# A hybrid RG-LRU and gated DeltaNet trunk on one core: new durations in the table from which a generator writes the order of the work

## The chip, the core and the metric

The kernel runs on one NeuronCore of one Trainium2 chip. The metric is the device time of one launch in microseconds. The engines are TensorE (PE, and PEld for its weight loads), VectorE (DVE), ScalarE (ACT), GpSimd (POOL) and SyncE (SP), which issues all the transfers. Each engine takes its instructions in the order in which the program lists them, and an instruction whose operand is not ready holds up everything behind it on that engine.

## The reference, cut to what matters

Two layers over 2048 frames of width 1024, then a last RMSNorm. Each layer is x = x + gate * Mixer(RMSNorm(x) * (1 + scale) + shift), where shift, scale and gate come from a linear map of SiLU(c).

```
# layer 0, RG-LRU
xb, zg = split(h @ in_w)                          # 1024 -> 2 * 1024
xb = causal_conv4(xb) + conv_b
r, i = sigmoid(blockdiag(xb) + gate_b)            # 8 blocks of 128 x 128
a = exp(-8 * r * softplus(-lam))
hseq = scan(h_t = a_t * h_{t-1} + sqrt(1 - a^2) * (i * xb))
out = (hseq * silu(zg)) @ out_w

# layer 1, gated DeltaNet, 8 heads of 128
q, k, v = silu(causal_conv4(h @ in_w[q, k, v]));  z, a_in, b_in = h @ in_w[z, a, b]
per chunk: A = strict_lower(beta * k k^T * decay);  T = (I + A)^-1
           v_new = T(beta v) - T(beta k e^g) S;  o = (q e^g) S + (q k^T * decay) v_new
           S = S * e_last + k_dec^T v_new
out = (rmsnorm(o) * silu(z)) @ out_w
```

All inputs and outputs are fp32.

## The kernel before

Every large matrix product is made of three products of fp32r halves (high by high, high by low, low by high), each 128x128 by 128x512, accumulated in a PSUM tile over eight blocks of 128: 24 products for one tile of 128x512. They are the line `pe.matmul` of `products` (L667); the tile is `mm` in the input projections and `mmo` in the output projections. A *job* is one such tile. The first layer has 64 jobs for its input and 32 for its output projection, the second 128 and 32. The tokens come in two halves `u` of 1024, each in two groups `i` of 512.

What hangs on a job of the first layer: ScalarE copies `mm` to `xe` (`extend`, L727; POOL copies the carry of four columns, L725 and L730), POOL makes the first tap of the convolution and VectorE the other three (`taps`, L715, the tile `xf1`); ScalarE rounds it to `xh` (L765), VectorE makes the rest `xl` (L768), and six gate products `pg` (L774) on TensorE use both. Then come the activations, the scan on VectorE (L805) and the product with the other branch (`tz`, L752). Beside that, `row_halves_thread` accumulates the condition columns on VectorE (`acc`, L412) and reduces them with small products (L280, L423); VectorE and POOL split the normalised input of the next half into `hh` and `hl` (L570, L576).

In the second layer a job of the kinds q, k and v goes through the same convolution (`xf`) to `qt`, `kt`, `vt` (L975). For a head, `key_thread` transposes the key on TensorE (`pk`, L1094), makes `pkk` (L1129) and the decayed matrix `ac`; `inverses_thread` inverts its 32x32 blocks by substitution on VectorE, 62 dependent steps (`ttmp`, `tblk`, L1249 and L1252); `levels_thread` merges them; `query_thread` makes `pqk` (L1214). `recurrence_thread` then goes over eight blocks `m` of 128 tokens for each half: two products `pp` with the state (L1369, L1370), `zt` on VectorE (L1378), `py` (L1386), `yt` on ScalarE (L1392), two products `pS` (L1398, L1399), and the new state on VectorE (L1411), which the next `pp` needs.

**What sets the order.** The program has no loops on the chip. Python threads (generators) describe the work, and the class `Weave` runs them at build time: each `yield "dve", 0.605` says that the next instructions take VectorE for 0.605 us by the table, each `yield slots[...]` asks for a buffer, each `yield ev(...)` waits for another thread. `run` always takes the thread that can start first by this reckoning, and among equals the one with the lower priority number; the recurrences have 0, the projections 9. What it takes is emitted, and so the four engines and the transfer queue each get their fixed order. Nothing of this reckoning is left at run time: there, semaphores make an instruction wait for its operands. So the table's numbers set where an instruction stands in its queue, and nothing else. The names in capitals are the commonest durations: STT and EV a 128x512 VectorE instruction, CP a 128x512 ScalarE copy, TR a 128x128 transpose, MM a 128x512 product and M4 a 128x128 fp32 product. LAG is the time from an instruction's end until its result counts as usable.

Buffers matter too: PSUM has two tiles each of `mm`, `tp`, `c` and `d`, so a job cannot start before the job two before it has been copied out.

## Time and profile before

| | |
|---|---|
| three runs | 1982.22, 1989.81, 1986.4 us; median 1986.4 |
| the profiled execution | 1980.38 us, span 1978.6 us |
| busy: PE, PEld | 1846.2 us (93%), 1500.3 us (76%) |
| busy: DVE, ACT, POOL | 1475.7 us (75%), 1046.7 us (53%), 724.1 us (37%) |
| DMA | 322.77 MB, mean 163 GB/s |
| granted TensorE clock | 0.985 |

A busy PE is a sum of modelled, overlapping durations, so what counts on TensorE is where it has nothing running, and what ended that idle time. In the views, "PE pg L774 <- DVE xl L768" reads: TensorE stood idle before an instruction of line 774 that writes `pg`, and the last thing to come was VectorE's `xl` of line 768. The chain that ended last goes through TensorE for 46% of the span, VectorE 21% and DMA 10%.

### The profile page before, as it was taken

Reading aid. Unit: us, or ns where it says so; the run is one execution under the profiler, and the core shown is the slowest. Engines: PE = TensorE matmul, PEld = TensorE weight load, DVE = VectorE, ACT = ScalarE, POOL = GpSimd, SP = SyncE. Lnnn points to the kernel's source line nnn. Section 1 sums busy time; section 2 is a strip of 40 time slices with the busy share of each in tenths; the row PEclk is TensorE's granted clock in tenths of the full one; section 3 lists DMA queues with packets and bytes.
Section 4 is the critical chain, followed back from the end, with each engine's and each line's share of the span. In section 5 each row is a group of like instructions: output and inputs, shape, how many; then the busy total and the mean of one; then the engine's idle time right before and its main releaser. Section 6 shows DMA issues by size and latency. Waiting matters only on the chain.

```text
span 1978.6 us, 31398 instructions
## 1 busy us (share of the span) xinstructions
PE 1846.2 (93%) x10286; PEld 1500.3 (76%) x10286; DVE 1475.7 (75%) x3171; ACT 1046.7 (53%) x2555; POOL 724.1 (37%) x1215
## 2 busy tenths in 40 slices
PE   6998889999998998898989999999999999999998
PEld 3776667787787777777777778777888888878887
DVE  6788798887644567778977898567778778877654
ACT  3655567666411236465555555555656566654321
POOL 4555664444200135345344544333333334311101
PEclk9999999999999999999999999999999999999999
DMA  8355655654578724547764457455465555577751
GB/s 334 103 157 158 223 168 169 200 178 153 175 198 210 225 74 140 145 114 176 189 161 130 119 125 191 128 147 147 119 152 147 131 133 140 149 219 221 225 186 64
DMA packets 511724, 322.77 MB, mean 163 GB/s; under 512 B 371268, under 2 KB 439236, under 8 KB 511560
## 3 DMA queue, kind: packets, MB, share of 16 engines
q1 hardware_dynamic: 511560, 320.77, 57.4%
q8 instruction: 81, 1.33, 0.3%
q14 instruction: 83, 0.68, 0.1%
HBM read 219.93 MB, written 100.73 MB: 162 GB/s over the span
## 4 chain that ended last, share of the span: by engine, by line
PE 46%; DVE 21%; DMA 10%; issue 6%; ACT 6%; POOL 5%; SPq 5%; DVEq 0%; POOLq 0%; ACTq 0%
PE mm L667 21%; PE mmo L667 12%; DVE xf L715 6%; DMA raw<-in_w 2%; DVE ttmp L1249 2%; DVE tblk L1252 2%; PE pg L774 1%; DMA xt<-x_d 1%; SPq L1187 1%; SPq L512 1%; DVE acc L412 1%; PE pp L1369 1%; PE pS L1398 1%; PE pkk L1129 1%; PE pS L1399 1%
## 5 line engine op out<-in xcount | busy, mean ns | idle before, releaser
L715 DVE SCALAR_TENSOR_TENSOR xf<-xe,cw_s,xf 128x512 f32<-128x512 f32 x384 | 331.4, 866 | 46.7 <-POOL xf L958 24.1
L649 POOL TENSOR_TENSOR wlo<-raw,whi 128x1024 fp32r<-128x1024 f32 x48 | 120.6, 2512 | 99.7 <-ACT whi L643 81.2
L1249 DVE TENSOR_TENSOR ttmp<-blk,tblk 128x60 f32<-128x60 f32 (+24 forms) x496 | 118.3, 238 | 24.9 <-DMA blk<-blk_d 11.5
L643 ACT CAST whi<-raw 128x1024 fp32r<-128x1024 f32 x96 | 100.4, 1045 | 64.5 <-DMA raw<-in_w 54.7
L1252 DVE TENSOR_TENSOR tblk<-tblk,ttmp 128x60 f32<-128x60 f32 (+24 forms) x496 | 122.3, 247 | 10.0 <-POOL tblk L1243 0.2
L730 POOL COPY carry<-xe 128x4 f32<-128x4 f32 x128 | 40.3, 315 | 239.2 <-ACT xe L727 237.1
L727 ACT COPY xe<-mm 128x512 f32<-128x512 f32 x128 | 73.9, 578 | 74.0 <-PE mm L667 73.0
L667 PE MATMUL mm<-hh_('in2', 0)_5201,whi 128*128 128x512 f32 x256 | 105.0, 410 | 4.1 <-ACT xe L727 4.1
L667 PE MATMUL mmo<-oh,yh 128*128 128x512 f32 x256 | 101.1, 395 | 7.8 <-DVE xr L922 7.2
L667 PE MATMUL mm<-hh_('in2', 1)_12203,whi 128*128 128x512 f32 x256 | 105.2, 411 | 2.8 <-ACT xe L727 2.8
L667 PE MATMUL mm<-hh_('in2', 0)_5424,whi 128*128 128x512 f32 x256 | 103.7, 405 | 2.1 <-ACT xe L727 1.5
L667 PE MATMUL mm<-hh_('in2', 0)_5201,wlo 128*128 128x512 f32 x256 | 105.3, 411 | 0.0
L667 PE MATMUL mm<-hl_('in2', 0)_5425,whi 128*128 128x512 f32 x256 | 104.9, 410 | 0.0
L667 PE MATMUL mm<-hl_('in2', 0)_5202,whi 128*128 128x512 f32 x256 | 104.6, 409 | 0.0
L667 PE MATMUL mm<-hh_('in2', 1)_12379,wlo 128*128 128x512 f32 x256 | 104.4, 408 | 0.0
L667 PE MATMUL mm<-hh_('in2', 1)_12203,wlo 128*128 128x512 f32 x256 | 104.4, 408 | 0.0
L667 PE MATMUL mm<-hh_('in2', 0)_5424,wlo 128*128 128x512 f32 x256 | 104.0, 406 | 0.0
L667 PE MATMUL mm<-hl_('in2', 1)_12204,whi 128*128 128x512 f32 x256 | 103.8, 405 | 0.0
L667 PE MATMUL mm<-hl_('in2', 1)_12380,whi 128*128 128x512 f32 x256 | 103.2, 403 | 0.0
L667 PE MATMUL mm<-hh_('in2', 1)_12379,whi 128*128 128x512 f32 x256 | 103.1, 403 | 0.0
L667 PE MATMUL mmo<-oh,oh 128*128 128x512 f32 (+1 forms) x264 | 102.0, 386 | 0.2 <-DVE tz L986 0.2
L667 PE MATMUL mmo<-ol,oh 128*128 128x512 f32 (+1 forms) x264 | 102.1, 387 | 0.0
(324 smaller groups left out, 5698.7 us busy)
## 6 DMA issues: line engine op xcount, KB each, us to landing
raw<-in_w SPq DMA_DIRECT2D x96, 512.0 KB, 4.2
araw<-in_ada_w SPq DMA_DIRECT2D x32, 512.0 KB, 4.4
xt<-x_d SPq DMA_DIRECT2D x32, 512.0 KB, 4.5
xt_d<-xb SPq DMA_DIRECT2D x192, 64.0 KB, 2.6
xk<-xt_d SPq DMA_DIRECT2D x24, 512.0 KB, 5.5
xt<-in_x SPq DMA_DIRECT2D x16, 512.0 KB, 4.9
ada<-in_ada_w SPq DMA_DIRECT2D x16, 512.0 KB, 9.1
y_d<-tz SPq DMA_DIRECT2D x32, 256.0 KB, 3.1
```

Source lines behind the costliest of these rows:

```text
L412: dve.scalar_tensor_tensor(acc, raw[:, k, :], ck, acc, ALU.mult, ALU.add)
L512: sp.dma_start(out=dst[c_], in_=tb[32 * c_:32 * c_ + 32])
L643: act.copy(hi, raw)
L649: pool.tensor_tensor(lo, raw, f(hi), ALU.subtract)
L667: pe.matmul(pt, lhsT=lhs[a][:, k, :], rhs=rhs[b][:, k, :], start=(k == 0 and n == 0), stop=(k == KT - 1 and n == 2))
L715: dve.scalar_tensor_tensor(xf, xe[:, 1 + j:1 + j + TC], wc[:, j:j + 1], xf, ALU.mult, ALU.add)
L727: act.copy(xe[:, 4:4 + TC], pt)
L730: pool.tensor_copy(out=carry, in_=xe[:, TC:TC + 4])
L774: pe.matmul(pg, lhsT=a[:, g, :], rhs=b, start=(q == 0), stop=(q == 2))
L1129: pe.matmul(pkk[:, b, :], lhsT=kc, rhs=kc, start=True, stop=True)
L1249: dve.tensor_tensor(tmp, blk[:, j, j + 1:32].unsqueeze(2).to_broadcast([P, r, c_]), t[:, j, 0:c_].unsqueeze(1).to_broadcast([P, r, c_]), A ...
L1252: dve.tensor_tensor(t[:, j + 1:32, 0:c_], t[:, j + 1:32, 0:c_], tmp, ALU.subtract)
```

## The change

The table of durations is replaced nearly everywhere, and TensorE's part of `Weave` gets two kinds of work. "pe" are the small products; "mm" the large ones, and an "mm" that comes behind a "pe" counts 0.087 us longer. Apart from the reckoning, only the matrix `middle` is moved: it was made by two POOL instructions at the start, in memory kept for the whole kernel, and is now made when the second layer's memory is opened, and `decay_thread` waits for it.

```
+    SWITCH = 0.087
+    ENGINE = {"mm": "pe"}
...
-                self.free[w[0]] = t + w[1]
-                th.t = t + w[1] + (w[2] if len(w) > 2 else self.LAG[w[0]])
+                dur = w[1]
+                if w[0] in ("pe", "mm"):
+                    if w[0] == "mm" and self.small:
+                        dur += self.SWITCH
+                    self.small = w[0] == "pe"
+                e = self.ENGINE.get(w[0], w[0])
+                self.free[e] = t + dur
+                th.t = t + dur + (w[2] if len(w) > 2 else self.LAG[e])
...
-    STT, EV, CP, TR, MM, M4 = 0.665, 0.605, 0.48, 0.109, 0.2163, 0.218
+    STT, EV, CP, TR, MM, M4 = 0.78, 0.61, 0.49, 0.112, 0.2275, 0.23
...
-            yield "pool", 0.14
+            yield "pool", 0.27
...
-        yield "dve", STT
+        yield "dve", 1.41
...
-            dur = 0.065 + r * c_ / 960.0
+            dur = 0.11 + r * c_ / 960.0
...
-                yield "act", 0.16
+                yield "act", 0.19
...
-    middle = cp.tile([P, P], F32, name="middle")
-    pool.tensor_copy(out=middle, in_=upper)
-    pool.tensor_scalar(middle[0:64, :], middle[0:64, :], -1.0, 0.0, ALU.add, ALU.add)
...
         enter("l2", "l2a")
+        middle = tile_([P, P], "middle", "middle")
+        pool.tensor_copy(out=middle, in_=upper)
+        pool.tensor_scalar(middle[0:64, :], middle[0:64, :], -1.0, 0.0, ALU.add, ALU.add)
+        w.set(ev("middle"), middle)
```

The four single prices are those of the carry copies in `extend` (0.14 to 0.27), the scan (0.665 to 1.41), a step of the substitution and `yt`. Left out are some thirty more prices of the same kind, most of them raised: the other VectorE instructions of the first layer from 0.605 to between 0.69 and 0.85, POOL's from 0.6 to 0.93 and the like, ScalarE's by a few hundredths, the four groups of small products in `levels_thread` from 0.38, 0.88, 0.4 and 0.9 to 1.1, 1.1, 1.0 and 1.1.

Line numbers below are those of each kernel's own text; up to L940 a line of the functions spoken of here stands 7 lines further down in the changed kernel, and from `decay_thread` on 12 or 13. The scan L805 is printed as SCALAR_TENSOR_TENSOR in the order and as TENSOR_TENSOR_SCAN in the profile.

How the order moves, first on VectorE in the first layer, around the fifteenth `xl`, from the last taps of its `xf1` to itself. Before:

```order
L715 SCALAR_TENSOR_TENSOR xf1_2238<-xe1_2217,cw1_s_97,xf1_2238 128x512 x2
L801 TENSOR_TENSOR tg_2127<-tg_2127,tg_2109 128x512
L805 SCALAR_TENSOR_TENSOR tg_2127<-th_2141,tg_2127 128x512
L412 SCALAR_TENSOR_TENSOR acc_2038<-araw_2247,c_col_92,acc_2038 128x512 x2
L801 TENSOR_TENSOR tg_2185<-tg_2185,tg_2177 128x512
L570 CAST hh_('in1', 1)_2265<-h_2286 128x512
L805 SCALAR_TENSOR_TENSOR tg_2185<-th_2196,hcar_104,tg_2185 128x512
L576 TENSOR_TENSOR hl_('in1', 1)_2266<-h_2286,hh_('in1', 1)_2265 128x512
L570 CAST hh_('in1', 1)_2265<-h_2292 128x512
L768 TENSOR_TENSOR xl_2316<-xf1_2238,xh_2299 128x512
```

And the same `xl` in the changed kernel:

```order
L722 SCALAR_TENSOR_TENSOR xf1_2269<-xe1_2240,cw1_s_94,xf1_2269 128x512
L577 CAST hh_('in1', 1)_2282<-h_2312 128x512
L759 SCALAR_TENSOR_TENSOR tz_2319<-tz_2319,mm_2244 128x512
L583 TENSOR_TENSOR hl_('in1', 1)_2283<-h_2312,hh_('in1', 1)_2282 128x512
L775 TENSOR_TENSOR xl_2342<-xf1_2269,xh_2324 128x512
```

The two scans and the two accumulations that stood between the last tap and `xl` now stand ahead of the taps; three instructions are left between.

Second on TensorE in the second layer, one step of a recurrence (`py`, then `pS`) in the second half of the tokens. Before:

```order
L1386 MATMUL py_14110<-zt_14095,ac_13111 128x128
L667 MATMUL mm_14098<-hh_('in2', 1)_12379,wlo_13712 128x512
L667 MATMUL mm_14098<-hh_('in2', 1)_12379,whi_13789 128x512
L667 MATMUL mm_14098<-hl_('in2', 1)_12380,whi_13789 128x512
L667 MATMUL mm_14098<-hh_('in2', 1)_12379,wlo_13712 128x512
L1398 MATMUL pS_14124<-yt_14115,kd_13021 128x128
L1399 MATMUL pS_14124<-yt_14115,at_13203 128x128
```

And the same step in the changed kernel:

```order
L1399 MATMUL py_14129<-zt_14120,ac_13085 128x128
L674 MATMUL mm_14075<-hl_('in2', 1)_12413,whi_13731 128x512
L674 MATMUL mm_14075<-hh_('in2', 1)_12412,wlo_13676 128x512
L674 MATMUL mm_14075<-hh_('in2', 1)_12412,whi_13731 128x512
L1411 MATMUL pS_14140<-yt_14132,kd_12983 128x128
L1412 MATMUL pS_14140<-yt_14132,at_13206 128x128
```

Three large products stand between `py` and `pS` where four stood.

More of the change, by code (lines that the diff above doesn't have):

```diff
@@ L75 @@
     LAG = {"pe": 0.2, "act": 0.3, "dve": 0.3, "pool": 0.2}
+    SWITCH = 0.087
+    ENGINE = {"mm": "pe"}
     def __init__(self):
         self.free = dict.fromkeys(("pe", "act", "dve", "pool", "sp", "dma"), 0.0)
+        self.small = True
         self.threads = []
@@ L108, in start @@
             return max(th.t, w.freed[last]) if last in w.freed else None
-        return max(th.t, self.free.get(w[0], 0.0))
+        return max(th.t, self.free.get(self.ENGINE.get(w[0], w[0]), 0.0))
     def run(self):
@@ L206, in trunk_kernel @@
     tags |= {t: ("l2", n) for t, n in {
-        "xe": 2, "xf": 2, "kt": KTN, "qt": QTN, "vt": 1, "ec": 3, "gr": 1, "ac": 4, "atn": 4, "kd": 4, "vn": 4,
+        "xe": 2, "xf": 2, "kt": KTN, "qt": QTN, "vt": 1, "ec": 3, "gr": 1, "middle": 1, "ac": 4, "atn": 4, "kd": 4, "vn": 4,
         "rq": 4, "nk": 4, "oo": 2, "tblk": 1, "ttmp": 1, "tf": 2, "zt": 2, "t2": 2, "yt": 2, "so": 2, "ro": 2,
@@ L210, in trunk_kernel @@
         "gs": 2, "eg": 2}.items()}
-    for t in ("xe", "xf", "vt", "ec", "gr", "ab", "gin", "gg", "spe", "spd"):
+    for t in ("xe", "xf", "vt", "ec", "gr", "middle", "ab", "gin", "gg", "spe", "spd"):
         tags[t] = ("l2a", tags[t][1])
@@ L457, in scale_thread @@
         put("ss", stok)
-        yield "dve", STT
+        yield "dve", 0.7
         dve.tensor_scalar(xt, xt, rs, None, ALU.mult)
@@ L559, in split_thread @@
         ttok = yield slots[tag]
-        yield "act", 0.665
+        yield "act", 0.71
         h = tile_([P, TC], tag, "h")
@@ L568, in split_thread @@
         else:
-            yield "dve", 0.33
+            yield "dve", 0.46
             dve.tensor_copy(out=hh[:, k, :], in_=h)
@@ L574, in split_thread @@
         else:
[L575 removed]
+            yield "dve", 0.75
             dve.tensor_tensor(hl[:, k, :], h, f(hh[:, k, :]), ALU.subtract)
@@ L728, in extend @@
         put("mm", mtok)
-        yield "pool", 0.14, 0.0
+        yield "pool", 0.27, 0.0
         pool.tensor_copy(out=carry, in_=xe[:, TC:TC + 4])
@@ L738, in conv1_thread @@
         ftok = yield slots["xf1"]
-        yield "pool", 0.76
+        yield "pool", 1.2
         xf = tile_([P, TC], "xf1", "xf1")
@@ L765, in gates_thread @@
         act.copy(xh, xf)
-        yield "dve", EV
+        yield "dve", 0.7
         xl = tile_([P, TC], "xr", "xl", F32R)
@@ L786, in gates_thread @@
         act.activation(tr, tr, AF.Exp, bias=sp4n[:, n:n + 1], scale=sp4n[:, n:n + 1])
-        yield "dve", EV, 0.13
+        yield "dve", 0.69, 0.13
         dve.scalar_tensor_tensor(th, tr, 1.0, th, ALU.add, ALU.mult)
-        yield "dve", EV
+        yield "dve", 0.69
         dve.scalar_tensor_tensor(tr, th, 2.0, th, ALU.subtract, ALU.mult)
-        yield "pool", 0.6, 0.0
+        yield "pool", 0.93, 0.0
         pool.tensor_scalar(th, th, -1.0, 1.0, ALU.mult, ALU.add)
-        yield "dve", EV
+        yield "dve", 0.85
         dve.scalar_tensor_tensor(ti, ti, 1.0, xf, ALU.add, ALU.mult)
@@ L806, in gates_thread @@
         put("th", htok)
-        yield "pool", 0.13
+        yield "pool", 0.42
         pool.tensor_copy(out=hcar[:, n:n + 1], in_=ti[:, TC - 1:TC])
@@ L810, in gates_thread @@
         tz, ztok = yield ev("tz", u, n, i)
-        yield "pool", 1.23
+        yield "pool", 1.42
         pool.tensor_tensor(tz, tz, ti, ALU.mult)
@@ L955, in conv2_thread @@
         ftok = yield slots["xf"]
-        yield "pool", 0.68
+        yield "pool", 0.72
         xf = tile_([P, TC], "xf", "xf")
@@ L1045, in decay_thread @@
         yield "pe", 1.1
+        middle = yield ev("middle")
         pgc = ps.tile([P, 3, NB * NH], F32, tag="tp", name="pgc")
@@ L1286, in levels_thread @@
         ctok = yield slots["c"]
-        yield "pe", 0.38
+        yield "pe", 1.1
         px = ps.tile([P, NTC, TB, 32], F32, tag="c", name="px")
@@ L1449, in outputs_thread @@
         for b in range(TB):
-            yield "act", 0.255, 0.0 if b < TB - 1 else 0.27
+            yield "act", 0.295, 0.0 if b < TB - 1 else 0.27
             act.activation(oo[:, b, :], oo[:, b, :], AF.Copy, scale=ro[:, b:b + 1])
```

28 lines of the change are left out of this document (13 added, 15 removed).

## Prediction

> **What bounds the kernel now.** I read the page first, then the stages, then who TensorE waited for, and last the order of time at the places where it waited longest.
>
> The page's span, busy shares and slices (TensorE):
>
> ```profile
> span 1978.6 us, 31398 instructions
> ...
> PE 1846.2 (93%) x10286; PEld 1500.3 (76%) x10286; DVE 1475.7 (75%) x3171; ACT 1046.7 (53%) x2555; POOL 724.1 (37%) x1215
> ...
> PE   6998889999998998898989999999999999999998
> ```
>
> TensorE is at work in 93% of the span, nothing else comes near, and the dips lie at the start, in the fourth to sixth digit and from the thirteenth to the twenty-first. The stages tell it in microseconds (columns: stage and length, then busy time of PE, PEld, DVE, ACT, POOL with their instructions, granted clock, DMA share, GB/s):
>
> ```profile
> 60.00:300.00 240.00, 209.07 (x852) 163.42 (x851) 202.52 (x238) 147.50 (x206) 143.84 (x137) 0.95 0.56 168
> 300.00:490.00 190.00, 184.79 (x806) 149.42 (x804) 159.63 (x199) 130.14 (x170) 84.55 (x97) 0.99 0.55 179
> 490.00:697.00 207.00, 195.92 (x841) 157.79 (x840) 113.79 (x150) 57.17 (x71) 30.16 (x36) 0.99 0.68 197
> 697.00:1240.00 543.00, 499.55 (x3175) 409.29 (x3174) 433.01 (x1149) 300.75 (x931) 239.93 (x437) 0.98 0.57 144
> 1240.00:1783.00 543.00, 528.02 (x3497) 436.77 (x3496) 412.05 (x1203) 329.60 (x1004) 178.15 (x412) 1.00 0.56 147
> 1783.00:1979.00 196.00, 188.45 (x971) 157.42 (x967) 113.88 (x151) 57.71 (x136) 21.53 (x56) 0.99 0.56 172
> ```
>
> The first two rows are the input projection of the RG-LRU layer, the third its output projection, the fourth and fifth the two halves of the DeltaNet layer, the last the final output projection. TensorE stands still for 240.0 - 209.1 = 31 us in the first row, 5 us in the second, 11 in the third, 543 - 499.6 = 43 us in the fourth, 15 in the fifth and 8 in the last. Only this standing time can be won by another order, since the products themselves stay; one row of the chain of waits prices them:
>
> ```profile
> 1832.16 139.53 PE mmo L667 x638
> ```
>
> 638 products with nothing waiting, the last 48 of them half as wide: 139.53 / (590 + 24) = 227 ns for one of 128x512. Below I count a place in TensorE's order in units of these 227 ns.
>
> Who TensorE waited for (us in total, times, longest):
>
> ```profile
> PE pg L774 <- DVE xl L768: 23.1, 13, 5.2
> ...
> PE pS L1398 <- ACT yt L1392: 9.1, 12, 1.6
> PE mm L667 <- ACT xe L727: 8.4, 5, 2.8
> PE pp L1369 <- DVE state L1411: 7.8, 6, 1.9
> ...
> PE pk L1094 <- DVE tblk L1252: 5.2, 4, 2.0
> PE adac L280 <- DVE acc L358: 4.8, 2, 2.5
> PE adapt L423 <- DVE acc L412: 3.9, 2, 2.8
> PE py L1386 <- DVE zt L1378: 3.9, 6, 1.6
> ...
> PE adapt L280 <- DVE acc L412: 3.4, 3, 1.7
> ```
>
> Most of it is one kind: a small product on TensorE stands in its in-order queue before VectorE (or ScalarE) has made its operand, and every large product behind it waits too. The sum of the rows with a VectorE or ScalarE cause here is 69.6 us.
>
> **The change, term by term.** All sums are against the profiled execution (1980.38 us, span 1978.6), which lies 6.0 us under the median of the three runs, 1986.4; I add the sum to that median, because after the change a median is compared too. The change adds no arithmetic and no transfer: TensorE has the same 8452 instructions, VectorE and the sync queue the same number. It moves them, moves two POOL instructions, and drops four loads of an activation table.
>
> Gate products (pg behind xl). The longest wait, in order of time on VectorE and then on TensorE:
>
> ```profile
> 272.93 0.75 DVE L715 SCALAR_TENSOR_TENSOR xf<-xe,cw_s,xf 128x512 f32<-128x512 f32 x1
> ...
> 275.46 2.55 DVE L412 SCALAR_TENSOR_TENSOR acc<-araw,c_col,acc 128x512 f32<-128x512 f32 x2
> ...
> 278.88 1.27 DVE L805 TENSOR_TENSOR_SCAN tg<-th,hcar,tg 128x512 f32<-128x512 f32 x1
> 280.07 0.66 DVE L576 TENSOR_TENSOR hl_('in1', 1)_2266<-h,hh_('in1', 1)_2265 128x512 fp32r<-128x512 f32 x1
> 280.65 0.41 DVE L570 CAST hh_('in1', 1)_2265<-h 128x512 fp32r<-128x512 f32 x1
> 280.99 0.68 DVE L768 TENSOR_TENSOR xl<-xf,xh 128x512 fp32r<-128x512 f32 x1
> ```
>
> ```profile
> 281.72 0.79 PE L774 MATMUL pg<-xl,gh 128*128 128x512 f32 x1 [5.16 <-DVE xl L768]
> 282.31 0.63 PE L774 MATMUL pg<-xh,gl 128*128 128x512 f32 x1
> ```
>
> The last tap of the convolution ends at 272.93 + 0.75 = 273.68, but xl, which TensorE stands waiting for, starts at 280.99: nine other VectorE instructions stand between them in the order, among them two of the accumulations L412 (2.55 us) and two scans. The generator had taps, accumulations and scans at 0.665 us each; the rows of a tap and an accumulation say otherwise (beside them a step of the inverse and an instruction with one operand in PSUM, for later):
>
> ```profile
> L715 DVE SCALAR_TENSOR_TENSOR xf<-xe,cw_s,xf 128x512 f32<-128x512 f32 x384 | 331.4, 866 | 46.7 <-POOL xf L958 24.1 <-POOL xf L741 17.0 <-POOL xe L721 2.2
> ...
> L1249 DVE TENSOR_TENSOR ttmp<-blk,tblk 128x60 f32<-128x60 f32 (+24 forms) x496 | 118.3, 238 | 24.9 <-DMA blk<-blk_d 11.5 <-DMA tt_d<-ttmp 2.4 <-POOL tblk L1243 1.6
> L412 DVE SCALAR_TENSOR_TENSOR acc<-araw,c_col,acc 128x512 f32<-128x512 f32 x56 | 50.6, 903 | 6.0 <-DMA araw<-in_ada_w 5.6
> ...
> L752 DVE SCALAR_TENSOR_TENSOR tz<-tz,mm 128x512 f32<-128x512 f32 x32 | 21.8, 680 | 11.2 <-ACT tz L750 8.4 <-issue 2.8
> ```
>
> 866 (L715) and 903 ns (L412) against 665, and 1.27 us for the scan at 278.88. With 0.78 (and 1.41 for the scan) the generator holds VectorE for longer, so the small product comes later among the large ones. At this place the order now leaves three VectorE instructions between tap and xl (by their rows L570 0.41, L752 0.68 and L576 0.66, 1.8 us instead of 7.3), and the 5.16 us should go. Over all 32 groups, the number of large products between the end of the projection and the pg that needs xl rises from 43.5 to 48.9 in the mean: 5.4 x 227 ns = 1.2 us more lead. If each of the 13 waits shrank by that, 13 x 1.2 = 15.6 us would go. But in the mean VectorE has as many instructions between tap and xl as before (2.6), and at nine of the 32 places the lead is shorter; priced place by place with the old times, new waits eat all and 1 us more. Between -15.6 and +1 I take -9, nearer to the first, because the longest wait is one that I can see go.
>
> Clock. After the 5.16 us the next two products last 0.79 and 0.63 us, and the granted clock of 60 to 300 us is 0.95: 5% of 240 us is 12 us. Fewer long waits give some of it back: 0 to -6, I take -2.
>
> Accumulations before the condition columns (L280, L423): 4.8 + 3.9 + 3.4 = 12.1 us in seven waits. Eight steps that are priced 0.115 us higher place the product 0.9 us later: up to -6; +2 if the longer lead only moves the column's users. I take -3.
>
> Key transposes (pk): 5.2 us in four waits behind tblk, the substitution inside the inverses. Its steps are 238 ns in the row L1249; the generator had 0.065 us plus a nanosecond per element and now has 0.11, still too little. The lead grows by 0.2 us in the mean, by over 1 us at most of the waiting places. From -8 to +6, I take -2.
>
> Recurrence, third product (pS behind yt). One step of it in order of time, on TensorE and then on ScalarE:
>
> ```profile
> 1399.84 0.38 PE L1386 MATMUL py<-zt,ac 128*128 128x128 f32 x2
> 1399.98 0.47 PE L667 MATMUL mm<-hh_('in2', 1)_12379,wlo 128*128 128x512 f32 x1
> 1400.30 0.39 PE L667 MATMUL mm<-hh_('in2', 1)_12379,whi 128*128 128x512 f32 x1
> 1400.52 0.40 PE L667 MATMUL mm<-hl_('in2', 1)_12380,whi 128*128 128x512 f32 x1
> ...
> 1400.99 0.38 PE L1398 MATMUL pS<-yt,kd 128*128 128x128 f32 x2
> ```
>
> ```profile
> 1400.26 0.28 ACT L1392 ACTIVATE yt<-py 128x128 f32<-128x128 f32 x1 [0.38 <-PE py L1386]
> ```
>
> pS starts 1400.99 - 1399.84 = 1.15 us after py, behind four large products; yt is done at 1400.54, so there are 0.45 us to spare. The generator now counts the first large product behind a small one as 0.087 us longer. That is real: it occupies 1400.30 - 1399.98 = 0.32 us here, the next 0.22. So it puts three products where four stood (72 of 120 places had four, now 63 have three), and 0.45 - 0.22 = 0.23 us are left. ScalarE is not always free:
>
> ```profile
>   PE py L1386: 30.2, 67
> ```
>
> In 67 of 128 cases ScalarE stood idle until py came; in the other 61 something else ran. If all 61 cost the lost product, 61 x 0.22 = +13 us; if the better table keeps ScalarE clear, the 9.1 us go. The twelve places that wait already lose 12 x 0.22 = 2.6; I take +3. The other two steps of the recurrence (py behind zt, 3.9 us; pp behind the state, 7.8) keep four products in most places, in the mean 0.07 and 0.12 us fewer: 120 x 0.19 = +23 at worst, -11.7 if all waits go, and I take 0, since neither table nor order says which.
>
> The rest at nothing, with what covers it. Exposed weight loads: the order has 550 returns from small to large products, before 555; five times 0.1 us is -0.5. Waits for PSUM (mm behind xe, 8.4 us): xe is priced 0.49 instead of 0.48, the distance between a bank's two uses is the same in the mean. Table loads:
>
> ```profile
> L797 ACT ACT_TABLE_LOAD x26 | 33.4, 1283 | 0.5
> ```
>
> 26 such loads before the square roots (53 in all) become 24 (49 in all): 4 x 1.283 = 5 us of ScalarE, which is 147.5 of 240 us busy there; between -5 and 0, taken as 0. The matrix `middle` is made by two POOL instructions that move from the kernel's start to the opening of the second layer, where POOL is busy 30.2 of 207 us; its user stands behind all of the decays' other work. Without that cover it would cost under 1 us.
>
> Sum: -9 - 2 - 3 - 2 + 3 + 0 = -13, so 1986.4 - 13 = 1973 us. 0.5% (10 us) is about what a measurement of this kernel can tell from no change, so this is just beyond it.
>
> **Rivals.**
>
> (A) The plan meets the chip. If nearer prices make most VectorE-caused waits go, half of the standing time in the two worst stages goes, (31 + 43)/2 = 37 us, with 6 us of clock: 1943. For it: the waits do name the instructions whose price was lowest against their rows. Against it: the leads in the second layer hardly grow (pk 0.2 us, the recurrence less than nothing).
>
> (B) Tight recurrences, slower. With three products behind py, a ScalarE that starts yt more than 0.23 us late stops TensorE; 61 of 128 cases are exposed: +13, and a third of the +23 of py and pp is +8: 1986 + 21 = 2007. It decides if the wait for yt doubles without the pg wait halving. Against it: at most places ScalarE starts yt at once.
>
> (C) Prices that change with the order. The row of xl (min/median/max) shows that one instruction has no one price:
>
> ```profile
> L768 DVE TENSOR_TENSOR xl<-xf,xh x32: 657/682/1745, 65.0 to 512.9; 128x512 fp32r<-128x512 f32 x32
> ```
>
> 657 to 1745 ns for the same tile, and the taps L715 take 866 ns where L752, with one operand in PSUM, takes 680. Something lengthens VectorE instructions with two SBUF operands by up to a microsecond, and a new order pairs them anew. The taps lose 384 x (866 - 680) = 71 us in all; a quarter more is 18 us of VectorE, of which I count the quarter of the taps that lies in 60 to 490 us (where VectorE is 362 of 430 us busy), 4.5 us, and as much for the other instructions there: 1986 + 9 - 5 (half of what the pg term wins) = 1990.
> The Trainium skill ("SBUF — State Buffer", section "Who interferes with whom") says that a VectorE instruction with two SBUF inputs and a GpSimd instruction that reads SBUF exclude each other for the whole of an instruction, so that the order of issue decides who waits. By that rule a table of means is right only for the order in which it was traced, which speaks against this change; the trace agrees as far as L715 and L752 differ.
>
> (D) It does nothing that shows: 550 against 555 returns, the same work, the waits only change places: 1986.
>
> **How the numbers follow.** My forecast (1973, its own range 1955 to 1990) 0.44; A 0.20; B 0.18; C 0.07; D 0.11. Faster by over 0.5% (under 1976.5): 0.26 of the forecast's 0.44 and A, 0.46. Slower (over 1996.3): B, a third of C and a little of the forecast, 0.23. The same: the remaining 0.31. The range reaches into A and B, leaving a tenth at either end: 1938 to 2010.
>
> **What would show it.** Right: the wait of pg for xl falls from 23.1 to about 14 us, none near 5; PE busy in 60 to 300 us rises above 209 of what is then a shorter stage, granted clock above 0.95; the wait of pS for yt rises from 9.1 to about 12 us; the DeltaNet halves stay within 10 us of 543 each. Wrong: pg waits as long elsewhere (then the lead was no lead, and VectorE itself is late), or the DeltaNet halves move by more than 10 us either way, which would mean that what I priced at 0 (py, pp, the order of VectorE in the inverses) decides. The last stage cannot tell: 140 of its 196 us are one unbroken run of products.

## The result, and the profile after

The changed kernel is slower. Four runs of each: 2039.75 us median (2032.41 to 2044.72) against 1984.31 us before, ratio 1.0272 with a 95% interval of 1.0245 to 1.0299. Predicted were 1973 us, between 1938 and 2010. The profiled execution took 2032.41 us, 52 us more than that of before.

The page of the changed kernel (span, busy times, TensorE by slices):

```profile
span 2030.7 us, 31435 instructions
...
PE 1871.2 (92%) x10286; PEld 1510.9 (74%) x10286; DVE 1483.3 (73%) x3171; ACT 1037.9 (51%) x2551; POOL 718.7 (35%) x1215
...
PE   6989889999999998998998898989999999989998
```

TensorE does the same products with 52 us more of span, and behind the start its eights now stand from the sixteenth digit to the twenty-seventh, and again at the thirty-sixth. By stages (same columns as in the prediction):

```profile
60.00:300.00 240.00, 213.40 (x878) 168.41 (x877) 210.18 (x243) 148.25 (x208) 142.23 (x140) 0.95 0.57 173
300.00:490.00 190.00, 184.26 (x800) 149.23 (x798) 160.64 (x197) 124.47 (x167) 84.94 (x98) 0.98 0.53 174
490.00:690.00 200.00, 190.81 (x813) 152.52 (x814) 104.34 (x140) 51.96 (x66) 29.09 (x33) 0.99 0.69 201
690.00:1275.00 585.00, 525.08 (x3335) 422.97 (x3335) 452.31 (x1183) 315.11 (x958) 248.82 (x448) 0.98 0.54 141
1275.00:1838.00 563.00, 532.01 (x3437) 437.94 (x3436) 404.12 (x1182) 317.53 (x986) 166.37 (x404) 0.97 0.52 137
1838.00:2031.00 193.00, 185.47 (x873) 154.61 (x871) 110.61 (x142) 55.70 (x128) 21.53 (x55) 0.99 0.53 164
```

Length less PE's busy time is TensorE's standing time. In the first half of the DeltaNet layer (fourth row) it is 585 - 525.1 = 60 us where it was 43, in the second half 31 where it was 15. The two rows of the first layer have 27 and 6 us, 31 and 5 before. Measured from the first large product of a stage to that of the next, the first input projection went from 465.5 to 459.2 us, and the two DeltaNet halves from 556.6 to 586.3 and from 531.4 to 561.9.

Who TensorE waited for in the changed kernel (us in total, times, longest; L674 is the old L667, L781 the old L774, L1411 the old L1398):

```profile
PE pS L1411 <- ACT yt L1405: 24.2, 24, 3.0
...
PE mm L674 <- ACT xe L734: 13.6, 5, 4.6
PE pk L1107 <- DVE kt L987: 10.6, 4, 4.3
PE mm L674 <- DVE tz L759: 9.3, 3, 4.0
PE pp L1382 <- DVE state L1424: 8.2, 8, 2.3
PE py L1399 <- DVE zt L1391: 7.4, 11, 1.5
PE adapt L287 <- DVE acc L419: 6.8, 2, 6.5
PE pqk L1227 <- DVE qt L987: 6.7, 6, 2.9
PE pg L781 <- DVE xl L775: 6.7, 9, 2.3
PE pk L1107 <- DVE ttmp L1262: 5.2, 3, 3.5
```

The wait of `pg` for `xl` fell from 23.1 to 6.7 us and its longest from 5.2 to 2.3. The wait of `pS` for `yt` rose from 9.1 to 24.2 us, and of the others in the second layer `pk`, `py` and `pqk` have more than before, while `pp` is about even. Two rows are of large products: `mm` behind `xe`, 8.4 before, and behind the first layer's `tz`. Before, the rows of `kt` and of that `tz` were:

```profile
PE pk L1094 <- DVE kt L975: 3.2, 4, 1.4
...
PE mm L667 <- DVE tz L752: 0.4, 1, 0.4
```

For the experiments I use one account, made from the starts of all matrix products in the trace: a product that starts over 0.15 us later than a dense row would have it (0.227 us behind a 128x512 product, 0.111 behind a 128x128 one, 0.06 behind a smaller) has waited, and the excess is booked to it. Runs of products at half clock (below) are booked apart. Before: 116.0 us in front of small products, 33.2 in front of large ones, 16.0 at half clock. After: 136.5, 50.3 and 24.1. Together 165.2 and 210.9: these 45.7 us are nearly all of the 52. The half clock is counted low in it. By the profile's clock records TensorE ran at half clock for 61.0 us before and 105.6 after; with the excess of every product that starts in these stretches booked to it, half clock takes 20.7 us before and 36.3 after, and the three columns together rise by 51.

### The profile page after: what moved, and what is told of

Its sections match the earlier page's. It is cut to its first block, busy times and chain, and to the rows that moved or that the text cites. A ratio compares the mean times of both kernels' runs of the same rounds, so it can differ in the third digit from the quotient of the medians.

```text
span 2030.7 us, 31435 instructions
## 1 busy us (share of the span) xinstructions
PE 1871.2 (92%) x10286; PEld 1510.9 (74%) x10286; DVE 1483.3 (73%) x3171; ACT 1037.9 (51%) x2551; POOL 718.7 (35%) x1215
## 4 chain that ended last, share of the span: by engine, by line
PE 37%; DVE 18%; DMA 17%; ACT 10%; SPq 7%; issue 6%; POOL 4%; DVEq 0%; POOLq 0%; ACTq 0%
PE mm L674 18%; PE mmo L674 10%; DVE xf L722 3%; DMA raw<-in_w 3%; DMA pq<-q_d 2%; SPq L1200 2%; DMA q_d<-tb 2%; SPq L519 1%; DVE tblk L1265 1%; PE pg L781 1%; DVE ttmp L1262 1%; DMA blk_d<-ac 1%; ACT junkq L1180 1%; DMA xt<-x_d 1%; ACT junk L1118 1%
## 5 line engine op out<-in xcount | busy, mean ns | idle before, releaser
L737 POOL COPY carry<-xe 128x4 f32<-128x4 f32 x128 | 38.8, 303 | 268.0 <-ACT xe L734 264.8
L674 PE MATMUL mm<-hh_('in2', 0)_5200,whi 128*128 128x512 f32 x256 | 104.1, 407 | 6.6 <-ACT xe L734 6.5
L674 PE MATMUL mm<-hh_('in2', 0)_5424,whi 128*128 128x512 f32 x256 | 105.9, 414 | 2.2 <-DVE tz L998 1.6
L674 PE MATMUL mm<-hh_('in2', 1)_12183,whi 128*128 128x512 f32 x256 | 106.2, 415 | 1.9 <-ACT xe L734 1.9
L674 PE MATMUL mmo<-oh,yh 128*128 128x512 f32 x256 | 101.0, 395 | 6.0 <-DVE xr L929 3.0
L674 PE MATMUL mm<-hh_('in2', 1)_12412,wlo 128*128 128x512 f32 x256 | 105.8, 413 | 0.0
L674 PE MATMUL mm<-hl_('in2', 1)_12184,whi 128*128 128x512 f32 x256 | 105.8, 413 | 0.0
L674 PE MATMUL mm<-hh_('in2', 1)_12183,wlo 128*128 128x512 f32 x256 | 105.8, 413 | 0.0
L674 PE MATMUL mm<-hh_('in2', 1)_12412,whi 128*128 128x512 f32 x256 | 105.4, 412 | 0.0
L674 PE MATMUL mm<-hl_('in2', 1)_12413,whi 128*128 128x512 f32 x256 | 105.4, 412 | 0.0
L674 PE MATMUL mm<-hh_('in2', 0)_5200,wlo 128*128 128x512 f32 x256 | 105.3, 411 | 0.0
L674 PE MATMUL mm<-hl_('in2', 0)_5425,whi 128*128 128x512 f32 x256 | 105.1, 411 | 0.0
L674 PE MATMUL mm<-hh_('in2', 0)_5424,wlo 128*128 128x512 f32 x256 | 105.0, 410 | 0.0
L674 PE MATMUL mm<-hl_('in2', 0)_5201,whi 128*128 128x512 f32 x256 | 104.8, 409 | 0.0
L674 PE MATMUL mmo<-oh,yl 128*128 128x512 f32 x256 | 101.2, 395 | 3.1 <-DVE yl L903 3.1
L674 PE MATMUL mmo<-oh,oh 128*128 128x512 f32 (+1 forms) x264 | 102.2, 387 | 0.0
```

Of the source, the lines that this page charges most:

```text
L674: pe.matmul(pt, lhsT=lhs[a][:, k, :], rhs=rhs[b][:, k, :], start=(k == 0 and n == 0), stop=(k == KT - 1 and n == 2))
L737: pool.tensor_copy(out=carry, in_=xe[:, TC:TC + 4])
```

## The experiments

Three theories stood at the start. Theory 1: the one large product that is lost between `py` and `pS` is what the recurrence loses. Theory 2 (theory E in the later texts): the other engines' prices do the harm. Theory 3: the order is a lottery, the old table is one that won, and any redraw loses. Theory S came later: the old table had TensorE too fast, so that each small product stood later than its operand, and this spare time took up what the other engines were late. In the table a time before stands only where it changes; rows below share it.

| run | table | us (beside: before) | ratio, 95% interval |
|---|---|---|---|
| e1_noswitch | changed kernel, no surcharge | 2025.55 (1988.79) | 1.0179 [1.0152, 1.0205] |
| e2_pe_prices | before, TensorE's new prices | 2072.03 | 1.0407 [1.0382, 1.0432] |
| e3_engines | changed kernel, TensorE's old prices | 2034.09 | 1.0219 [1.0198, 1.0239] |
| e4_yt_later | changed kernel, `yt` usable later | 2034.95 | 1.0234 [1.0216, 1.0252] |
| p1_mm | before, MM 0.2165 | 2002.12 (1987.95) | 1.0071 [1.0044, 1.0098] |
| p2_stt | before, STT 0.667 | 1987.63 | 1.0005 [0.9989, 1.0022] |
| p3_cp | before, CP 0.482 | 1987.09 | 0.9988 [0.9971, 1.0006] |
| p4_m4 | before, M4 0.2185 | 1986.73 | 1.0000 [0.9981, 1.0020] |
| f1_lag | changed kernel, LAG up by half | 2025.24 (1987.99) | 1.0198 [1.0174, 1.0222] |
| f2_levels | before, the four level groups | 1990.45 | 1.0024 [1.0007, 1.0040] |
| f3_pe_const | before, TensorE's constants | 2057.67 | 1.0354 [1.0335, 1.0373] |
| f4_dve | before, VectorE's new prices | 2019.92 | 1.0175 [1.0143, 1.0206] |
| g5_switch | before, the surcharge | 2006.84 (1986.97) | 1.0095 [1.0070, 1.0120] |
| g6_mm2275 | before, MM 0.2275 | 2025.74 | 1.0198 [1.0176, 1.0221] |
| f7_mm2055 | before, MM 0.2055 | 1964.75 | 0.9892 [0.9869, 0.9916] |
| e6_yt_sooner | before, `yt` usable sooner | 1987.78 | 1.0003 [0.9990, 1.0016] |
| h1_mm1947 | before, MM 0.1947 | 1978.04 (1986.82) | 0.9951 [0.9933, 0.9969] |
| h2_lag | before, LAG up by half | 1982.40 | 0.9987 [0.9970, 1.0005] |

### The two halves of the change

e1_noswitch, the changed kernel with

```
-    SWITCH = 0.087
+    SWITCH = 0.0
```

> The changed kernel with the price of an exposed weight load set from 0.087 to 0; every other new price stays. In the order, pS again stands behind four large products in most places (84 of 120; 63 had three). Theory 1 (the lost product between py and pS lets every late yt stop TensorE): the wait of pS for yt falls from 24.2 us to about 9, and the time from 2040 to 2000 or below. Theory 2 (the loss comes from the new prices of VectorE, ScalarE and POOL): 2025 to 2045, since those stay. Theory 3 (any new table draws another order, good or bad by chance): anything from 1980 to 2050, without relation to the wait of pS.

Measured 2025.55 us. Four products stand between `py` and `pS` in 84 places again, and the wait of `pS` for `yt` is 16.6 us instead of 24.2. The time is 14 us below the changed kernel's, of the 55 it had lost: little more than a redraw for no reason can do (0.7%, below). Theory 1 had the wait near 9 us and the time at 2000 or below.

e2_pe_prices is the kernel before with all of TensorE's new prices and nothing else; e3_engines the changed kernel with TensorE's prices put back:

```
e2:  -  STT, EV, CP, TR, MM, M4 = 0.665, 0.605, 0.48, 0.109, 0.2163, 0.218
     +  STT, EV, CP, TR, MM, M4 = 0.665, 0.605, 0.48, 0.112, 0.2275, 0.23
     +  SWITCH = 0.087;  levels 1.1, 1.1, 1.0, 1.1
e3:     STT, EV, CP, TR, MM, M4 = 0.78, 0.61, 0.49, 0.109, 0.2163, 0.218
        SWITCH = 0.0;  levels 0.38, 0.88, 0.4, 0.9
```

The price of a group of three gate products (0.71 in the change, three times MM before it) goes with TensorE's prices, here and in f3 below.

> Only TensorE's new prices (0.2275, 0.23, 0.112, the 0.087 behind small products, the groups of the inverse); VectorE, ScalarE and POOL keep the old ones. pS stands behind three products in 64 places. Theory 1: slow like the change, 2020 to 2045, with a wait of pS for yt above 18 us. Theory 2: near before, 1975 to 1995. Theory 3: anything.

> The other half: new prices for VectorE, ScalarE and POOL, TensorE's old ones and no 0.087. pS stands behind four products in most places (65 of 120). Theory 1: no loss, 1970 to 1995, and the gate products of the first layer wait less than the 23.1 us of before. Theory 2: slow, 2020 to 2045. Theory 3: anything.

TensorE's prices alone cost more than the whole change (2072.03 us), and the other engines' alone cost 45 us. They do it at different places. The waits in e2:

```profile
PE pg L781 <- DVE xl L775: 27.0, 21, 4.5
PE pS L1411 <- ACT yt L1405: 23.7, 28, 2.6
```

and in e3:

```profile
PE py L1399 <- DVE zt L1391: 17.3, 20, 2.8
PE mm L674 <- ACT xe L734: 15.2, 8, 3.6
```

In e2 the small products wait (`pg` worse than before the change, `pS` as in the changed kernel). In e3 the large products wait: 52.5 us in the account against 33.2 before and 27.4 in e2; of the small ones `py` rose most. Theory 2 had e2 near the time before, and theory 1 had no loss in e3, so neither holds as it stands.

### Is it the lost product?

e4_yt_later (changed kernel) and e6_yt_sooner (kernel before) change one number, the time until `yt` counts as usable:

```
e4:  -  yield "act", 0.19              e6:  -  yield "act", 0.16
     +  yield "act", 0.19, 0.5275           +  yield "act", 0.16, 0.2
```

> The changed kernel with all its prices; only the result of yt counts as usable 0.2275 us later, so that four products stand between py and pS in 63 places where three stood. Theory 1: the wait of pS for yt falls from 24.2 to about 10 us, and with it most of the loss: 2000 to 2015. Theory 2: 2030 to 2045, with a shorter wait of pS and as much waiting elsewhere. Theory 3: anything.

> The kernel before with one number changed: yt counts as usable 0.2 us after its end instead of 0.3, so that three large products instead of four stand between py and pS in 65 places; all else keeps its price. Theory 1 (the lost product is what the recurrence loses): 2000 or more, the wait of pS for yt from 9 to over 18 us. Theory S (the lost product is one of many places that lose spare time): 1985 to 1998, pS behind yt up by 5 to 9 us, the others as before.

e4 puts four products back in 63 places. Its time is 5 us below the changed kernel's, but the intervals overlap (1.0216 to 1.0252 and 1.0245 to 1.0299), and the wait of `pS` is 18.7 us, where theory 1 had about 10. In e6, three products stand between `py` and `pS` in 65 places, as in the changed kernel, all else being old:

```profile
PE pS L1398 <- ACT yt L1392: 11.1, 15, 1.6
PE py L1386 <- DVE zt L1378: 8.4, 8, 1.6
```

11.1 us instead of 9.1 for `pS`, 8.4 instead of 3.9 for `py`, and the time does not change (0.9990 to 1.0016). Theory 1 falls: by itself the lost product costs nothing that can be measured.

### Is it a lottery?

p1 to p4 change one constant of the kernel before by a thousandth to four thousandths, which redraws thousands of rows of the order:

```
p1: MM 0.2163 -> 0.2165    p2: STT 0.665 -> 0.667
p3: CP 0.48 -> 0.482       p4: M4 0.218 -> 0.2185
```

> The kernel before with one price changed by 0.2 ns: a large product 0.2165 instead of 0.2163 us. The price means nothing, but the generator draws another order from it (4427 of 7527 rows of TensorE's order change place or buffer). Theory 3 (the order is a draw, and the old table was kept because its draw is good on this chip): clearly slower than before, 2000 to 2040, in the second layer above all. Theory 1 and 2 (the prices matter for what they say): within 10 us of before, since it says the same; pS keeps four products (76 of 120).

> The kernel before with the price of a 128x512 VectorE instruction at 0.667 instead of 0.665 us. Theory 3: another draw, 2000 to 2040. Theories 1 and 2: within 10 us of before.

> The kernel before with the price of a 128x512 ScalarE copy at 0.482 instead of 0.48 us. Theory 3: another draw, 2000 to 2040. Theories 1 and 2: within 10 us of before.

> The kernel before with the price of a small fp32 product at 0.2185 instead of 0.218 us. Theory 3: another draw, 2000 to 2040; the four of this set then scatter by 10 us or more among themselves. Theories 1 and 2: within 10 us of before.

Three of four redraws stay within 0.3% and one loses 0.7%. Theory 3 falls as a reason for 2.7%, but it leaves a rule for the rest: a single kernel that is 0.7% off shows nothing about the price that was changed in it. 0.7% is the largest of four redraws and no bound.

### Which of the prices

f2_levels, f3_pe_const and f4_dve are the kernel before with one group of new prices each:

```
f2:  levels 0.38, 0.88, 0.4, 0.9 -> 1.1, 1.1, 1.0, 1.1
f3:  TR, MM, M4 = 0.112, 0.2275, 0.23;  SWITCH = 0.087;  gate products 0.71
f4:  STT, EV = 0.78, 0.61;  scan 1.41;  substitution 0.11 + r * c_ / 960;  first layer 0.69 to 0.85
```

> The kernel before with only the four groups of small products in levels_thread priced 1.1, 1.1, 1.0, 1.1 instead of 0.38, 0.88, 0.4, 0.9. Theory S: these 1.74 us for each of 16 heads and halves were the largest stretch by which the plan of TensorE ran ahead of the chip; without it part of the loss of the kernel with TensorE's new prices (2072) appears, 2000 to 2030, with the levels' own waits up by 5 us or more. If only the price of the large product and its surcharge matter: 1978 to 1995.

> The kernel before with TensorE's constants alone (large product 0.2275, fp32 product 0.23, transpose 0.112, 0.087 behind a small one), the four level groups at their old prices. Theory S: the constants carry most of the 2072 of all of TensorE's new prices, 2020 to 2060, pS behind 3 products and its wait for yt over 15 us. If the level groups carry it: 1980 to 2000.

> The kernel before with VectorE's new prices alone (taps 0.78, scan 1.41, substitution step 0.11 plus its size, the others of the first layer 0.7 to 0.85); TensorE, ScalarE and GpSimd keep theirs. Theory E: these carry the loss of all three engines' prices (2034), so 2015 to 2040 with waits of the large products over 65 us and the first layer faster by 5. If GpSimd's and ScalarE's prices carry it: 1975 to 2000. Theory S alone, by which dearer VectorE steps put the products later and so give spare time: 1970 to 1985.

TensorE's constants carry 3.5% and VectorE's prices 1.75%. The level groups do nothing beyond the noise above, so the first guess of theory S, that they carry part of it, was wrong. g5_switch and g6_mm2275 part the constants:

```
g5:  SWITCH = 0.087, MM = 0.2163        g6:  no SWITCH, MM = 0.2275
```

> The kernel before with only the surcharge of 0.087 us for a large product behind a small one (and the matrix middle made later); all prices old. TensorE's constants as a whole cost 70 us. Theory S (the plan's TensorE was too fast by about a tenth and that difference was the spare time): the surcharge is 551 x 0.087 = 48 us of 133 us by which those constants lengthen the plan's TensorE time, so 36% of 70: 2005 to 2020. Theory M (the price of the large product alone is a tuned value): 1980 to 1995.

> The kernel before with only the price of the large product raised from 0.2163 to 0.2275, which is what the profile shows for one (227 ns). Theory S: 72 of the 133 us, 54% of the loss: 2018 to 2035, with pS behind yt over 15 us and pg behind xl over 25. Theory L (the loss is the surcharge's alone): 1980 to 2000.

19.9 and 38.8 us, together 59 of the 70 of f3, both times inside what theory S had. The 1.0% of g5 is not far beyond a redraw. The waits in g6, where nothing but the price of the large product was raised:

```profile
PE pg L774 <- DVE xl L768: 20.8, 17, 4.8
PE pS L1398 <- ACT yt L1392: 16.7, 16, 2.8
...
PE pk L1094 <- DVE kt L975: 13.6, 11, 3.4
PE py L1386 <- DVE zt L1378: 11.5, 9, 2.0
```

16.7 us for `pS` (9.1 before), 13.6 for `pk` behind `kt` (3.2), 11.5 for `py` (3.9). `pg` behind `xl` did not come as theory S had it: 20.8 us, where it had over 25 and the kernel before has 23.1. One number, set to what the trace shows for such a product, brings as long waits in front of small products as the changed kernel has (148.9 us in the account against its 136.5), and none in front of large ones (33.8, 33.2 before).

### The sign

f7_mm2055 and h1_mm1947 move the same number the other way:

```
f7:  MM 0.2163 -> 0.2055        h1:  MM 0.2163 -> 0.1947
```

> The kernel before with only the price of the large product lowered from 0.2163 to 0.2055, the other way by as much. Theory S: spare time grows, pS behind yt and pg behind xl fall below 9 and 23 us, the time is the same or lower, 1965 to 1995. Theory M (0.2163 is a tuned optimum, and any other order this far away loses): 2010 to 2030.

> The kernel before with the price of the large product lowered twice as far, from 0.2163 to 0.1947. Theory S without a limit (each 5% of it is worth 20 to 40 us): 1930 to 1950. Theory S with a limit: at this price the generator's own reckoning has TensorE idle for 98 us (38 in the kernel before, 56 at 0.2055, 111 with VectorE's new prices), because VectorE has become its bound in places, and the waits of the large products come back as they did with VectorE's new prices (over 60 us against 41): 1965 to 2005, no better than 0.2055.

f7 is faster than the kernel before by 1.1%, the best version of all, and beyond what the redraws did. Its page, and three of its waits:

```profile
span 1960.6 us, 31383 instructions
...
PE 1850.0 (94%) x10286; PEld 1508.1 (77%) x10286; DVE 1482.0 (76%) x3171; ACT 1041.2 (53%) x2555; POOL 725.0 (37%) x1215
```

```profile
PE pg L774 <- DVE xl L768: 14.6, 12, 7.3
...
PE pS L1398 <- ACT yt L1392: 5.5, 10, 1.0
...
PE mm L667 <- ACT xe L727: 3.9, 5, 1.5
```

h1 is faster than before by 0.5%, and its gain is 0.6% less than that of f7. Both are no more than a redraw can do, so that a still lower price stops helping rests on the waits alone:

```profile
PE mm L667 <- ACT xe L727: 15.8, 9, 3.6
...
PE pg L774 <- DVE xl L768: 6.9, 8, 2.4
PE mm L667 <- DVE tz L986: 5.5, 6, 1.5
PE mm L667 <- DVE tz L752: 5.0, 2, 2.8
PE pS L1398 <- ACT yt L1392: 4.9, 13, 0.6
```

The small products wait still less (`pg` 6.9 us), but the rows of the large ones are back: 15.8 behind `xe`, 5.5 and 5.0 behind the two `tz`. The account of all these runs, in us (small and large products, half clock):

| run | small | large | half clock |
|---|---|---|---|
| h1, MM 0.1947 | 96.5 | 45.0 | 17.1 |
| f7, MM 0.2055 | 103.1 | 24.7 | 19.7 |
| before, MM 0.2163 | 116.0 | 33.2 | 16.0 |
| g6, MM 0.2275 | 148.9 | 33.8 | 24.5 |
| f3, all of TensorE's constants | 174.9 | 30.7 | 22.8 |
| e2, all of TensorE's prices | 184.4 | 27.4 | 23.9 |
| changed kernel | 136.5 | 50.3 | 24.1 |
| f4, VectorE's prices alone | 129.2 | 52.4 | 20.3 |
| e3, VectorE's, ScalarE's, GpSimd's | 136.7 | 52.5 | 25.0 |

The first column rises with each step by which TensorE's price rises, from 96.5 to 184.4. The spare time itself can be seen in part. At `pS` it can't: from the end of the instruction that made `yt` to the start of `pS` the median is 0.45 us before and 0.22 in g6, f3, e2 and the changed kernel, but it is 0.22 in e6 too, which loses nothing, and 0.45 in f7, which gains. This median says how many products stand between. At `pk`, whose operand comes from a longer chain, it moves with the price: from the end of the newest `kt` to the first `pk` that reads it the median is 0.69 us in h1, 0.55 in f7, 0.42 before (0.36 to 0.45 in p1 to p4 and f2) and 0.15 in g6. The second column has another cause: it is 48.5 to 52.5 in all six runs with VectorE's new prices, 24.7 to 38.8 in twelve of the fourteen without (45.0 in h1 and 42.0 in h2, below). The generator's own reckoning (the starts that it plans while it writes the order, no time of the chip) has something in common there with h1: it leaves TensorE idle for some 100 us in e3, f4 and h1, against some 40 before. But f7 has nearly 60 us by that reckoning and no such waits, and the changed kernel has them with some 45, so the reckoning is a hint and no proof.

### A fixed amount instead

f1_lag (changed kernel) and h2_lag (kernel before):

```
-    LAG = {"pe": 0.2, "act": 0.3, "dve": 0.3, "pool": 0.2}
+    LAG = {"pe": 0.3, "act": 0.45, "dve": 0.45, "pool": 0.3}
```

> The changed kernel with LAG raised by half (pe 0.3, act 0.45, dve 0.45, pool 0.3); all prices stay. Theory S (spare time): the old table priced TensorE too fast, so each small product stood later than its operand and the difference took up what the engines were late; the new TensorE prices took that away. Then larger lags give it back: 1990 us or less, the wait of pS for yt from 24 to under 9, py for zt from 7 to under 4, the waits of the large products unchanged near 72. Theory E (the other engines' prices put evacuations and projections late): 2020 to 2045, the large products' waits stay and longer leads only shift the recurrence.

> The kernel before with only LAG raised by half (pe 0.3, act 0.45, dve 0.45, pool 0.3): the spare time comes as a fixed amount per operand (pS behind five products in most places instead of four) instead of as a share of the time. If a fixed amount serves as well: 1955 to 1980, pS behind yt under 5 us. If only a share serves, because an engine that is late by more than the fixed amount catches up only where TensorE is slower than the plan: 1982 to 2005. In the changed kernel the same edit won 14 us.

Neither does much. In f1 theory S missed: it had 1990 us or less, `pS` behind `yt` under 9 us and `py` behind `zt` under 4, and measured are 2025 us, 16.8 and 14.5 (24.2 and 7.4 without the edit). The time lies where theory E had it. In h2 nothing can be measured (0.9970 to 1.0005), though five products stand behind `py` and the account has 5.7 us in front of `pS` instead of 12.8; the large products wait longer, 42.0 us against 33.2. The lag also puts off the copy out of PSUM behind the last product, so the test is not clean. That a fixed amount cannot serve is not shown, and why it did not help `py` in f1 stays open.

### One place

Here is one place of the changed kernel where a few tenths of a microsecond are not enough (start, duration, engine; in order of time, rows left out):

```profile
1476.63 0.38 SPq L1174 DMA_DIRECT2D pq<-q_d  x1
...
1476.96 1.28 ACT L1100 ACTIVATE ec<-ec,gc 128x128 f32<-128x128 f32 x4 [0.27 <-POOL ec L1096]
...
1478.05 0.38 PE L1399 MATMUL py<-zt,ac 128*128 128x128 f32 x2
1478.15 0.39 ACT L1464 ACTIVATE oo<-oo,ro 128x128 f32<-128x128 f32 x1
...
1478.19 0.48 PE L674 MATMUL mm<-hh_('in2', 1)_12412,whi 128*128 128x512 f32 x1
...
1478.51 0.39 PE L674 MATMUL mm<-hl_('in2', 1)_12413,whi 128*128 128x512 f32 x1
...
1478.74 0.40 PE L674 MATMUL mm<-hh_('in2', 1)_12412,wlo 128*128 128x512 f32 x1
...
1480.50 0.31 ACT L1180 ACTIVATE junkq<-pq 128x128 bf16<-128x128 f32 x1 [1.57 <-DMA pq<-q_d]
...
1481.78 0.26 ACT L1405 ACTIVATE yt<-py 128x128 f32<-128x128 f32 x1
...
1482.10 0.80 PE L1411 MATMUL pS<-yt,kd 128*128 128x128 f32 x2 [2.96 <-ACT yt L1405]
```

`py` has ended by 1478.4, three large products follow, and `pS` should start near 1479.0. But ScalarE, which has to make `yt`, has the sums `junkq` ahead of it in its order and stands for 1.57 us until the transfer `pq` has landed, 3.9 us after its issue at 1476.63. The sums and one other instruction then fill ScalarE until `yt` at 1481.78, and TensorE stands for 2.96 us. The table counts 1.13 + 256 KB / 360 KB per us + 0.92 = 2.8 us for such a transfer. All 32 of them, from issue to landing:

```profile
DMA to landing us min/median/max: 2.8/3.4/5.2
```

2.8 us is the shortest. The change moved the engines' prices towards their traced means, but left these transfers at what is their minimum. By theory S a TensorE that is priced too fast makes up for such things wherever they come from, since the chip then reaches the small product later than planned. That the transfers' price is a large part of the loss was not tried.

## Why the prediction was wrong, point by point

**What bounds the kernel** held in the main: TensorE's standing time decides, and the 45.7 us of the account are nearly the whole loss. But only 20.5 of them came in front of small products, and 17.1 in front of large ones.

**`pg` behind `xl`, -9**: right in sign and too small. The wait fell by 16.4 us, past the -15.6 I had as an end. The first input projection became only 6.3 us shorter: in it the wait of large products for `tz` rose from 0.4 to 9.3 us, and one of 6.5 us came in front of a condition product (`adapt`). What won is VectorE's prices: alone they make this stage 5.7 us shorter (459.8 in f4), and TensorE's alone make it 8.6 us longer (474.1 in e2).

**Clock, -2**: wrong in sign. The granted clock of 60 to 300 us is 0.95 as before, and half clock took 8 us more over the whole kernel by the account, 16 by the clock records.

**Accumulations, -3**: the three rows sum to 10.6 us (6.8 of them quoted above), 12.1 before. Little came of it.

**`pk` behind `tblk`, -2**: in the account `pk` went from 11.6 to 17.1 us. The wait for `tblk` left the list, and those for `kt` (3.2 to 10.6) and `ttmp` (1.5 to 5.2) rose.

**`pS` behind `yt`, +3**: it came to +15. The working was right for the edit that I looked at, one product fewer, as e6 shows (+2.0 us of waits). I had bounded it at +13 by places where ScalarE was at something else, but took that the rest of the order would stay. g6, without the surcharge, has three products there about as often as e6 (62 and 70 places in the traces), and yet 16.7 us of this wait against 11.1.

**`py` and `pp`, 0**: `pp` is about even (16.9 us in the account before, 15.2 after), `py` +6, within the +23 that I had as the worst case.

**The rest at nothing** is where it failed. Its line on returns from small to large products prices only the surcharge's count; and nowhere does the sum have a term for MM 0.2163 to 0.2275. I took that as a correction towards the 227 ns of the row and gave it no cost. It is the largest single term, 2.0% by g6, and with the surcharge (1.0%) and the other constants 3.5%. In g6, beside `pS`, its waits stand in rows to which the sum gave nothing: `pk` behind `kt` (3.2 to 13.6) and `py` behind `zt` (3.9 to 11.5). And the line on PSUM (`mm` behind `xe`) found the distance between a bank's two uses the same in the mean and took the waits as unchanged. Large products wait 17 us longer in the account, and VectorE's prices alone do that (52.4 us in f4). Less of it is `xe` (8.4 to 13.6) than the first layer's `tz` (0.4 to 9.3), which reads `mm` too and which the sum does not name; in f4 `xe` is 7.5 and that `tz` 8.1. Why VectorE's prices bring these waits stays open.

The two halves do not add: 3.5% or 4.1% for TensorE's side and 1.75% or 2.2% for the other make 2.7% together. With VectorE dear too, its small products move back (the first column falls from 184.4 in e2 to 136.5), while the large products keep the new waits.

**The rivals.** B had the sign and its time, 2007, was the nearest, but its mechanism, three products behind `py`, is not the cause: e6 has it and loses nothing. A had it the wrong way round: nearer prices made most waits longer. C had VectorE's taps lose more in the new order; they take 845 ns after and 866 before. D falls with the 52 us. The test that I had written down, that the DeltaNet halves would move by more than 10 us if what was priced at 0 decides, is the one that came true.

## What to carry to other kernels

In a generator that writes a fixed order, the table of durations is not only a forecast; it also sets spare time. Here the best price of the engine that bounds the kernel was some per cent too fast (0.2055 for a product of 0.227 us), so that on the chip small products come up later than planned and their operands have more time. Setting that one price to its traced value cost 2.0%. Dearer prices for VectorE went with longer waits of the large products; why is not shown. Whether the same holds for another kernel has to be tried: move one price both ways, and give a single order no weight unless it differs by more than redraws for no reason do, 0.7% in the worst of four here.

## What the hardware showed

During the 2.96 us wait above the granted clock (the third column from the right) fell to half, and it was half for some 6 us after it:

```profile
1470.00:1479.00 9.00, 9.00 (x56) 7.77 (x54) 8.73 (x28) 6.55 (x20) 2.43 (x4) 1.00 0.75 213
1481.00:1481.50 0.50, 0.00 (x0) 0.00 (x0) 0.00 (x0) 0.50 (x4) 0.00 (x0) 0.81 0.02 3
1481.50:1482.00 0.50, 0.00 (x0) 0.00 (x0) 0.00 (x0) 0.50 (x5) 0.00 (x0) 0.50 0.00 0
1482.00:1484.00 2.00, 1.90 (x7) 1.71 (x8) 1.35 (x5) 1.11 (x5) 1.41 (x3) 0.50 0.00 0
1484.00:1486.00 2.00, 2.00 (x7) 1.61 (x6) 0.79 (x3) 0.49 (x2) 0.03 (x1) 0.50 0.54 104
1486.00:1488.00 2.00, 2.00 (x8) 1.71 (x8) 1.13 (x5) 0.37 (x1) 0.00 (x0) 0.50 1.11 278
1488.00:1490.00 2.00, 2.00 (x13) 1.74 (x12) 0.95 (x5) 1.32 (x7) 0.00 (x0) 0.96 0.82 257
```

0.81 is the mean of the half microsecond from 1481.0, so the clock fell at about 1481.3, some 2.2 us after the last product had ended and before the next one started. Large products started 0.43 us apart at half clock instead of 0.23. So a wait of 3 us cost almost as much again behind it (an estimate: 6 us at about half the rate). By the clock records the changed kernel has 21 such stretches and the kernel before 16. The Trainium skill ("TensorE: Matmul & The Clock Gate", section "What's actually happening") says that the clock halves after an idle window of about 3.4 us and comes back after as long a busy one; here it halved 2.2 us into a wait, and came back after some 6 us of dense products.
